# Attention in a decoder trunk: maximum, softmax, values and copies of o by halves of the queries, and Q and K of the eighth pair moved into the Q/K phase

## The chip, the cores and the metric

The kernel runs on one core of one Trainium2 chip. The core has five engines with a program each: TensorE (PE, matrix products; its weight loads are listed apart as PEld), VectorE (DVE), ScalarE (ACT), GpSimd (POOL) and SyncE (SP, which here only issues DMAs). They meet through semaphores. The metric is the device time of one execution in microseconds. A profile comes from one further execution.

## The reference

Two layers work on x of 1024 tokens × 1024 channels, in fp32: a short gated convolution and a dilated attention, each followed by a SwiGLU feed-forward (FFN). The attention has 16 heads of 64 channels. Each head has three branches (window, dilation) = (128, 1), (512, 4), (2048, 16); each branch looks back over a band of keys, with a bias by distance, and the branches are weighted by their own sums of exponentials:

```python
h = rms_norm(x, mix_norm[i])
qkv = (h @ w_qkv).reshape(bsz, seq, 3, N_HEADS, HEAD_DIM)
for window, dilation in BRANCHES:
    o, l = dilated_branch(q, k, v, rel_bias, window, dilation)   # output, log of the sum of exponentials
    ...
alpha = jax.nn.softmax(jnp.stack(lses, axis=0), axis=0)
o = jnp.sum(alpha[..., None] * jnp.stack(outs, axis=0), axis=0)
x = x + o.reshape(bsz, seq, D_MODEL) @ w_out
x = x + swiglu(rms_norm(x, ffn_norm[i]), w_gate, w_up, w_down)
```

Since the weights alpha are exponentials of the branches' log sums, the three branches are one softmax over all their keys together. The kernel computes it so: one maximum, exponentials of everything, one sum.

## The kernel before, in words

**Products in two parts.** fp32 factors are split into a high part, which ACT rounds (L145), and the low part, which DVE subtracts (L146). A product is then three matmuls: high·high, high·low, low·high. `product` (L373 to L375) does it plainly. The larger products go through `Strassen` units: seven products of combined halves in place of eight, with DVE forming the combinations of raw weights (L193), PE multiplying (L571 to L573), and ACT and DVE adding the results up into `part` (L577, L581).

**The stages.** The convolution and its FFN come first (to 938 us). Then `QueryKey.mix` computes Q and K for `QK_PAIRS = 7` of the eight pairs of heads as Strassen units (938 to 1095 us). Each result is scaled and split (L1140, L1142, L1145, L1148) and goes to DRAM by POOL's DMAs. After the first value tiles the attention runs from 1123.8 to 1412.3 us in 17 slots, and the rest of the output projection and the second FFN follow.

**A slot.** `slot(n)` (L1717) has two halves. The first does the scores of head n (L1574, L1575) in eight steps. The second does the values of head n−1 (L1647). For n up to `LAG = 13` the softmax of head n−1 runs within the first half: five subtractions of the maximum on DVE (L1636), each followed by its exponential on ACT (L1637). From slot 13 on, a head's softmax runs in the second half of its own slot, and from slot 14 on scores and values are interleaved. The maximum of a head is taken on DVE (L1599, L1620 to L1625) and over the partitions by one POOL instruction of 1024 columns (L1628). Values are accumulated in two PSUM banks, one for each half of the queries; the weights hold 64 columns of ones beside the 64 of v, so that the sums of exponentials come out in the same product. Then ACT takes the logarithm of the sums (z, L1670) and copies o (L1671), for both halves after all values.

**Names.** lf and lh are the scores of the branch of dilation 4 (lh for the second half of the queries alone), ld and lp those of the other tiles of keys (lp for the block before); ka, qa, ql are K, Q and Q's low part; kca is K by residue; vx holds the values of one pair of heads; oin is a pair's finished output read back from DRAM; x<-spill are rows of x read back.

**Dense steps.** Between the pieces of a slot a generator `fill` puts further products on PE, and the table `DENSE` gives how many of its steps each slot takes: value tiles of the groups 1 to 3 (120 steps), Q and K of pair 7 (36 steps), then the first half of the output projection, `out_product(0)` (64 steps). With the numbers of before the output projection begins in slot 12. It takes the outputs of pairs 0 to 3 as split oin, adds its results to x (L492), and loads the x rows when it first takes a weight. A slot can also take a `hook`: in slot 11 it splits the four oin.

**Orders that are fixed.** Every engine carries its instructions out in the order of the program. SP issues, among others, K and Q (L1546 to L1552), the biases (L1468, L1469), vx (L1534, L1536), oin (L1799), x rows (L1811) and raw weights (L159). `load_values` brings in vx for the two heads of a pair one after the other, into a buffer of [ones between v of the even and v of the odd head]; vx has one buffer, so the load of a head's part waits until the last values that use it.

```python
vx = scope["pool"].tile([128, 16, 192], F32, name="vx", tag="vx", bufs=1)
nc.vector.memset(vx[:, :, 64:128], 1.0)
DENSE = (13,) * 13 + (16, 13, 12, 11)
```

Of the kernel before, what the change touches and what calls it, by code (L numbers as in the profile page):

```python
# [10 lines left out]
F32 = mybir.dt.float32  # L11
# [9 lines left out]
H = 16  # L21
# [80 lines left out]
def trunk(ctx: ExitStack, tc: tile.TileContext, x, gains_in, cwi, ck, cwo, wqkv, wo, relb,  # L102
# [8 lines left out]
    def page(name, dt=F32):  # L111
        return pages.tile([128, 1024], dt, name=name, tag="page", bufs=PAGES)
# [6 lines left out]
    def bank():  # L119
        return psum.tile([128, 512], F32, name="bank", tag="bank")  # L120
# [14 lines left out]
    def split(src, dst=None, eng=nc.vector):  # L135

        w = src.shape[1]
        if dst is None:
            if w <= HALF:
                t = page("w", F32R)  # L140
                dst = t[:, :w], t[:, HALF:HALF + w]
            else:
                dst = page("w_hi", F32R)[:, :w], page("w_lo", F32R)[:, :w]
        hi, lo = dst
        nc.scalar.activation(hi, src, AF.Copy)  # L145
        eng.tensor_tensor(out=lo, in0=src, in1=hi, op=ALU.subtract)  # L146
        return hi, lo

    raw_src, raw_tile, raw_state = [], {}, [0]
    ops, made, op_state = [], {}, [0, 0]
# [13 lines left out]
    def ensure(upto):  # L166
        while op_state[0] < min(upto + 1, len(ops)):
            key = ops[op_state[0] + 1][0] if op_state[0] + 1 < len(ops) else None
            if key in sums_of:
                sums_of.pop(key)()  # L170
            made[op_state[0]] = ops[op_state[0]][1]()
            op_state[0] += 1

    def take(key, ahead=1):
        i = op_state[1]
# [1304 lines left out]
    def attention(norm, qk):  # L1480
# [47 lines left out]

        def load_values(p):
            src = vdram[p // 2]  # L1530
            for a in range(2):
                off = src.offset + p % 2 * 128 + a * 64
                dims = slice(128 * a, 128 * a + 64)
                nc.sync.dma_start(vx[:, 0:8, dims], bass.AP(src.tensor, off, [[256, 128], [128 * 256, 8], [1, 64]]))  # L1534
                for h in range(2):
                    nc.sync.dma_start(vx[:, 8 + 4 * h:12 + 4 * h, dims],  # L1536
                                        bass.AP(src.tensor, off + 512 * 256 * h, [[1024, 128], [256, 4], [1, 64]]))

        def load_kq(n):

# [20 lines left out]
        def scores(p, a, st):  # L1561
# [63 lines left out]
            nc.vector.tensor_tensor(out=m[:, HALF:], in0=m[:, HALF:], in1=lp[:, HALF:], op=ALU.max)  # L1625
            mb = page("mb")
            st["mb"] = mb
            nc.gpsimd.partition_all_reduce(mb, m, 128, bass_isa.ReduceOp.max)  # L1628
            yield

        def softmax(st):
            lf, lh, ld, lp, mb = (st[n] for n in ("lf", "lh", "ld", "lp", "mb"))
            for dst, m in ((lf, mb), (lh, mb[:, HALF:]), (ld, mb),
                           (view(lp, 8, [[32, 16], [1, 24]]), view(mb, 8, [[32, 16], [1, 24]])),
                           (lp[:, HALF:], mb[:, HALF:])):
                nc.vector.tensor_tensor(out=dst, in0=dst, in1=m, op=ALU.subtract)  # L1636
                nc.scalar.activation(dst, dst, AF.Exp)  # L1637
                yield

        def values(p, a, st):  # L1640
            lf, lh, ld, lp = (st[n] for n in ("lf", "lh", "ld", "lp"))
            acc = [bank(), bank()]
            kd = [[128, 4], [1, 32]]
            b1 = [[32, 16], [1, 8]]

            def mm(ih, off, dims, u, rhs, first=False, last=False):
                nc.tensor.matmul(view(acc[ih], off, dims), vx[:, u, 64 * a:64 * a + 128], rhs,  # L1647
                                 start=first, stop=last)

            for ih in range(2):  # L1650
# [4 lines left out]
            for r4 in range(4):  # L1655
                mm(1, r4 * 32, kd, 12 + r4, view(lh, r4 * 32, kd))
                if r4 % 2:
                    yield
            for j in range(8):
                off = (j % 4) * 8  # L1660
                mm(j // 4, off, b1, j, view(ld, blk(j), b1), last=False)
                if j:
                    mm(j // 4, off, b1, j - 1, view(lp, blk(j), b1), last=j % 4 == 3)
                yield
            o, z = st["o"], st["z"]
            n0 = slice(64 * a, 64 * a + 64)
            z0 = slice(64 - 64 * a, 128 - 64 * a)
            for ih in range(2):
                s = slice(ih * HALF, (ih + 1) * HALF)
                nc.scalar.activation(z[n0, s], acc[ih][z0], AF.Ln)  # L1670
                nc.scalar.activation(o[n0, s], acc[ih][n0], AF.Copy)  # L1671
            yield

        def finish(p):

# [38 lines left out]
        put_off, ending, due = [], [], [iter(())]  # L1714
        OZ, acts = {}, {}

        def slot(n, dense, ndense, late=0, hook=iter(())):  # L1717

            def other(k):
                for _ in range(k):  # L1720
                    next(dense, None)

            p, a = divmod(n, 2)
# [5 lines left out]
            if n + 1 < H:  # L1729
                load_kq(n + 1)  # L1730
                bias[n + 1] = load_bias(n + 1)
            if n:
# [67 lines left out]
            return raw  # L1800

        def split_attended(raw):
            return {p: split(t) for p, t in raw.items()}

        def out_product(g, ps, acts):
            for n in range(KT):
# [29 lines left out]
                        yield from value_tiles(g, j)  # L1836
            yield from out_product(0, range(AO), first)

        def halves():
            for q, t in done.items():  # L1840
                first[q] = split(t)
                yield

        dense = fill()
        for n in range(H):
# [8 lines left out]
        run(dense)  # L1854
        return acts


# [178 lines left out]
```

## Time and profile before

| | |
|---|---|
| time, median of 3 runs | 2103.54 us (2102.79 to 2103.99) |
| the profiled execution's own time | 2105.08 us |
| its span | 2103.3 us |
| Q/K phase | 938 to 1095 us |
| first value tiles | 1095 to 1123.8 us |
| attention, 17 slots | 1123.8 to 1412.3 us |
| a slot, 1 to 9 | 16.8 to 17.7 us |
| slots 10, 11, 12, 13, 14 | 18.1, 17.3, 18.9, 20.9, 19.7 us |

The profile page gives for each engine its busy time, its share of the span and its number of instructions. A row of instruction groups reads: line, engine, operation, output<-input, shape, count | total us, mean ns of one | idle time of the engine just before them, and what ended it. A row of waits reads: engine, tile and line that waited <- engine, tile and line waited for: total us, how often, the longest. A row of time stretches has for each engine the busy time and the instructions. DMA rows of SP and POOL show when the engine issued, not when the data arrived.

### The profile page before, as it was taken

What the parts mean: (1) busy time and instruction counts of PE and PEld (TensorE: products, weight loads), DVE (VectorE), ACT (ScalarE), POOL (GpSimd) and SP (SyncE); (2) the same over time, 40 slices, a digit from 0 to 9 for tenths busy, and PEclk for the clock granted to TensorE, in tenths of its full rate; (3) what the DMA queues carried; (4) which work ended last, traced back from release to release, by engine and by line L of the source; (5) the groups of instructions that cost most, each with busy time, mean ns of one, the idle gap of its engine ahead of it and who ended that gap; (6) DMA issues with size and microseconds to landing.
All of it is one profiled execution on the core that took longest, in us unless ns stands there. A gap on an engine that the chain in (4) does not pass through costs nothing. (4 is left out here: it accounts for less than half of the span.)

```text
span 2103.3 us, 30766 instructions
## 1 busy us (share of the span) xinstructions
PE 2083.1 (99%) x10990; PEld 1792.2 (85%) x10990; DVE 1746.1 (83%) x3264; ACT 1013.7 (48%) x1852; POOL 240.0 (11%) x336
## 2 busy tenths in 40 slices
PE   9999999999999999999999999999999999999998
PEld 7788888888888888887789999988788888888887
DVE  8898769988888788968984778987998888888886
ACT  7433427444444454445553566555544434456433
POOL 1000000110101010010223232211011001001000
PEclk9999999999999999999999999999999999999999
DMA  7322643233333467452658788955223323368432
GB/s 216 100 96 71 230 135 76 101 105 111 102 105 110 145 201 208 133 159 65 232 201 209 161 202 210 250 165 154 71 87 108 107 99 113 110 194 245 158 96 80
DMA packets 141495, 300.70 MB, mean 143 GB/s; under 512 B 48236, under 2 KB 54462, under 8 KB 141344
## 3 DMA queue, kind: packets, MB, share of 16 engines
q1 hardware_dynamic: 107488, 201.94, 32.4%
q0 software_dynamic: 26224, 82.11, 12.6%
q10 hardware_dynamic: 7632, 14.70, 1.9%
q8 instruction: 87, 1.43, 0.3%
q14 instruction: 64, 0.52, 0.1%
HBM read 208.42 MB, written 82.93 MB: 139 GB/s over the span
## 5 line engine op out<-in xcount | busy, mean ns | idle before, releaser
L573 PE MATMUL bank<-b,w 128*128 128x512 f32 x1980 | 772.5, 390 | 5.4 <-DVE w L146 5.2
L571 PE MATMUL bank<-b,w 128*128 128x512 f32 x1980 | 772.3, 390 | 2.3 <-ACT w L145 1.1
L572 PE MATMUL bank<-b,w 128*128 128x512 f32 x1980 | 771.9, 390 | 0.6 <-DVE b L882 0.6
L573 PEld LDWEIGHTS bank<-b,w 128*128 128x128 f32 x1980 | 372.0, 188 | 87.5 <-DVE w L146 10.5
L571 PEld LDWEIGHTS bank<-b,w 128*128 128x128 f32 x1980 | 372.3, 188 | 80.3 <-ACT w L145 1.9
L572 PEld LDWEIGHTS bank<-b,w 128*128 128x128 f32 x1980 | 372.3, 188 | 76.6 <-DVE b L882 1.2
L145 ACT ACTIVATE w<-combo 128x512 fp32r<-128x512 f32 (+2 forms) x492 | 251.5, 541 | 238.9 <-DVE combo L193 219.7
L146 DVE TENSOR_TENSOR w<-combo,w 128x512 fp32r<-128x512 f32 (+2 forms) x492 | 279.8, 582 | 37.8 <-ACT w L145 37.0
L577 ACT ACTIVATE part<-bank 128x512 f32<-128x512 f32 x189 | 112.5, 595 | 383.9 <-PE bank L573 378.7
L146 DVE TENSOR_TENSOR w<-raw,w 128x512 fp32r<-128x512 f32 (+2 forms) x345 | 194.4, 585 | 36.5 <-ACT w L145 36.5
L581 DVE TENSOR_TENSOR part<-part,bank 128x256 f32<-128x256 f32 (+1 forms) x369 | 173.1, 499 | 31.9 <-PE bank L573 17.3
L145 ACT ACTIVATE w<-raw 128x512 fp32r<-128x512 f32 (+2 forms) x345 | 168.5, 531 | 47.8 <-PE bank L573 12.2
L373 PE MATMUL bank<-w_hi,w 128*128 128x512 f32 (+1 forms) x400 | 151.0, 378 | 0.1
L375 PE MATMUL bank<-w_hi,w 128*128 128x512 f32 (+1 forms) x400 | 149.3, 373 | 0.7 <-DVE w L146 0.7
L374 PE MATMUL bank<-w_lo,w 128*128 128x512 f32 (+1 forms) x400 | 149.0, 373 | 0.0
L801 DVE TENSOR_TENSOR x<-x,bank 128x512 f32<-128x512 f32 x136 | 92.9, 683 | 28.7 <-PE bank L573 28.7
L492 DVE TENSOR_TENSOR x<-x,bank 128x512 f32<-128x512 f32 (+1 forms) x104 | 66.7, 644 | 59.8 <-PE bank L375 58.9
L193 DVE TENSOR_TENSOR combo<-raw 128x512 f32<-128x512 f32 (+1 forms) x174 | 112.6, 648 | 0.0
L375 PEld LDWEIGHTS bank<-w_hi,w 128*128 128x128 f32 x400 | 75.3, 188 | 14.8 <-DVE w L146 1.6
L564 DVE TENSOR_TENSOR b<-hin,b 128x512 fp32r<-128x512 f32 x126 | 79.5, 686 | 9.4 <-ACT b L563 9.4
L373 PEld LDWEIGHTS bank<-w_hi,w 128*128 128x128 f32 x400 | 75.5, 189 | 12.3 <-ACT w L145 0.5
L374 PEld LDWEIGHTS bank<-w_lo,w 128*128 128x128 f32 x400 | 75.5, 189 | 11.9
(234 smaller groups left out, 3377.0 us busy)
## 6 DMA issues: line engine op xcount, KB each, us to landing
hin<-part SPq DMA_DIRECT2D x126, 256.0 KB
raw<-in_ffn_w_gate SPq DMA_DIRECT2D x44, 512.0 KB
raw<-in_ffn_w_up SPq DMA_DIRECT2D x44, 512.0 KB
part<-sum POOLq DMA_DIRECT2D x72, 256.0 KB, 2.3
raw<-in_ffn_w_down SPq DMA_DIRECT2D x48, 384.0 KB
raw<-in_attn_w_qkv SPq DMA_DIRECT2D x27, 512.0 KB
raw<-in_conv_w_in SPq DMA_DIRECT2D x24, 512.0 KB
part<-part POOLq DMA_DIRECT2D x36, 256.0 KB, 2.6
```

The costliest lines, as they stand in the source:

```text
L145: nc.scalar.activation(hi, src, AF.Copy)
L146: eng.tensor_tensor(out=lo, in0=src, in1=hi, op=ALU.subtract)
L193: eng.tensor_tensor(out=c, in0=a, in1=b, op=op)
L373: nc.tensor.matmul(b, whi[:, a], ahi[:, s], start=first, stop=False)
L374: nc.tensor.matmul(b, whi[:, a], alo[:, s], start=False, stop=False)
L375: nc.tensor.matmul(b, wlo[:, a], ahi[:, s], start=False, stop=last)
L571: nc.tensor.matmul(b, hi[:, a], bhi, start=start and k == 0, stop=False, skip_group_check=True)
L572: nc.tensor.matmul(b, hi[:, a], blo, start=False, stop=False, skip_group_check=True)
L573: nc.tensor.matmul(b, lo[:, a], bhi, start=False, stop=k == n - 1, skip_group_check=True)
L577: nc.scalar.activation(t, b, AF.Copy)
L581: nc.vector.tensor_tensor(out=t, in0=t, in1=b, op=ALU.add)
L801: nc.vector.tensor_tensor(out=X[n][:, half(h)], in0=X[n][:, half(h)], in1=b, op=ALU.add)
```

## The change

- `QK_PAIRS` is 8: the Q/K phase does the eighth pair as an eighth Strassen unit, and the 36 dense steps of pair 7 leave `fill`. `DENSE` has new numbers (184 steps in all), and the output projection's first half now begins in slot 11.
- The oin of pairs 0 and 1 are loaded and split in slot 9, those of pairs 2 and 3 in slot 10 (`OIN`), after the slot's K, Q and bias loads.
- The all-reduce of the maximum is two instructions of 512 columns, the first issued as soon as half a of the queries has its maximum. The softmax has seven steps of at most 512 columns, half a first, where there were five.
- The values do half a of the queries to its end, with its z and o, and then half b.
- vx is laid out as [ones, v of the even head, v of the odd head] repeated, so z and o change places, and both heads' values come in three DMAs with rows of 512 bytes, where there were six with rows of 256.
- During the attention a split's low part is not issued at once but put on a list, which is emptied ahead of the next dense step (`flush_lows`).

```diff
-QK_PAIRS = 7
+QK_PAIRS = 8
-FILL = (("v", 0), ("v", 1), ("v", 2), ("v", 3), ("qk", 7))
-DENSE = (13,) * 13 + (16, 13, 12, 11)
+FILL = (("v", 0), ("v", 1), ("v", 2), ("v", 3))
+OIN = LAG - 3
+DENSE = (11,) * 9 + (10, 10) + (11, 11, 14, 10, 10, 9)
...
-        eng.tensor_tensor(out=lo, in0=src, in1=hi, op=ALU.subtract)
+        low = lambda: eng.tensor_tensor(out=lo, in0=src, in1=hi, op=ALU.subtract)
+        if behind[0]:
+            lows.append(low)
+        else:
+            low()
...
+        flush_lows()
         ensure(i + ahead)
+        if i + 1 > state0:
+            flush_lows()
...
-        vx = scope["pool"].tile([128, 16, 192], F32, name="vx", tag="vx", bufs=1)
-        nc.vector.memset(vx[:, :, 64:128], 1.0)
+        vx = scope["pool"].tile([128, 16 * 192 + 64], F32, name="vx", tag="vx", bufs=1)
+        nc.vector.memset(view(vx, 0, [[192, 17], [1, 64]]), 1.0)
...
-            for a in range(2):
-                off = src.offset + p % 2 * 128 + a * 64
-                dims = slice(128 * a, 128 * a + 64)
-                nc.sync.dma_start(vx[:, 0:8, dims], bass.AP(src.tensor, off, [[256, 128], [128 * 256, 8], [1, 64]]))
-                for h in range(2):
-                    nc.sync.dma_start(vx[:, 8 + 4 * h:12 + 4 * h, dims],
-                                        bass.AP(src.tensor, off + 512 * 256 * h, [[1024, 128], [256, 4], [1, 64]]))
+            off = src.offset + p % 2 * 128
+            nc.sync.dma_start(view(vx, 64, [[192, 8], [1, 128]]),
+                              bass.AP(src.tensor, off, [[256, 128], [128 * 256, 8], [1, 128]]))
+            for h in range(2):
+                nc.sync.dma_start(view(vx, (8 + 4 * h) * 192 + 64, [[192, 4], [1, 128]]),
+                                  bass.AP(src.tensor, off + 512 * 256 * h, [[1024, 128], [256, 4], [1, 128]]))
...
+                    mb = page("mb")
+                    st["mb"] = mb
+                    nc.gpsimd.partition_all_reduce(mb[:, :HALF], m[:, :HALF], 128, bass_isa.ReduceOp.max)
                 yield
...
-            nc.gpsimd.partition_all_reduce(mb, m, 128, bass_isa.ReduceOp.max)
+            nc.gpsimd.partition_all_reduce(mb[:, HALF:], m[:, HALF:], 128, bass_isa.ReduceOp.max)
...
-            for dst, m in ((lf, mb), (lh, mb[:, HALF:]), (ld, mb),
+            a, b = half(0), half(1)
+            for dst, m in ((lf[:, a], mb[:, a]), (ld[:, a], mb[:, a]),
                            (view(lp, 8, [[32, 16], [1, 24]]), view(mb, 8, [[32, 16], [1, 24]])),
-                           (lp[:, HALF:], mb[:, HALF:])):
+                           (lf[:, b], mb[:, b]), (lh, mb[:, b]), (ld[:, b], mb[:, b]), (lp[:, b], mb[:, b])):
...
             for ih in range(2):
+                acc[ih] = bank()
                 for r4 in range(4):
...
+                for r4 in range(4 * ih):
+                    mm(1, r4 * 32, kd, 12 + r4, view(lh, r4 * 32, kd))
...
+                for j in range(4 * ih, 4 * ih + 4):
...
+                nc.scalar.activation(z[n0, half(ih)], acc[ih][n0], AF.Ln)
+                nc.scalar.activation(o[n0, half(ih)], acc[ih][o0], AF.Copy)
                 yield
...
-            if n == LAG - 2:
-                done.update(load_attended(range(AO)))
-            hook = halves() if n == LAG - 2 else iter(())
-            slot(n, dense, DENSE[n], 3 if n == H - 2 else 0, hook)
+            ps = {OIN - 1: (0, 1), OIN: (2, 3)}.get(n, ())
+            hook = halves(ps)
+            slot(n, dense, DENSE[n], 3 if n == H - 2 else 0, hook, ps)
```

On SP, this is slot 11 before, from the next head's K (ka) to the x rows, which slot 12's first dense step asks for:

```order
L1546 DMA ka<-kq_1_2926 64x1024
L1547 DMA ka<-kq_1_2926 64x1024
L1534 DMA vx<-vdram_95 128x8x64
L1536 DMA vx<-vdram_95 128x4x64 x2
L1534 DMA vx<-vdram_95 128x8x64
L1536 DMA vx<-vdram_95 128x4x64 x2
L1551 DMA qa<-kq_0_2925 64x1024 x2
L1552 DMA ql_10192<-kq_0_2925 64x1024
L1468 DMA bias<-tables 128x1x361
L1469 DMA bias<-tables 128x1x349
```

```order
L1551 DMA qa<-kq_0_2925 64x1024 x2
L1552 DMA ql_10193<-kq_0_2925 64x1024
L1468 DMA bias<-tables 128x1x361
L1469 DMA bias<-tables 128x1x349
L1811 DMA x<-spill_77 128x1024
L1811 DMA x<-spill_78 128x1024
L1811 DMA x<-spill_79 128x1024
```

Between the two pieces stand only the two loads of the next slot's ka. After, the same place:

```order
L1559 DMA ka<-kq_1_2926 64x1024
L1560 DMA ka<-kq_1_2926 64x1024
L1546 DMA vx<-vdram_95 128x8x128
L1549 DMA vx<-vdram_95 128x4x128 x2
L1564 DMA qa<-kq_0_2925 64x1024 x2
L1565 DMA ql_10353<-kq_0_2925 64x1024
L1482 DMA bias<-tables 128x1x361
L1483 DMA bias<-tables 128x1x349
L1829 DMA x<-spill_77 128x1024
L1829 DMA x<-spill_78 128x1024
L1829 DMA x<-spill_79 128x1024
```

The vx loads are three in place of six, and the x rows stand right behind the second bias, one slot's loads earlier.

On ACT, this is the end of slot 13 before: the softmax of head 13, then z and o of head 12's values, one pair of rows for each half of the queries:

```order
L1637 ACTIVATE lf<-lf 128x1024
L1637 ACTIVATE lh<-lh 128x512
L1637 ACTIVATE ld<-ld 128x1024
L1637 ACTIVATE lp<-lp 128x16x24
L1637 ACTIVATE lp<-lp 128x512
L145 ACTIVATE w<-raw 128x512
L1670 ACTIVATE z<-bank 64x512
L1671 ACTIVATE o<-bank 64x512
L1670 ACTIVATE z<-bank 64x512
L1671 ACTIVATE o<-bank 64x512
```

After, the same place:

```order
L1684 ACTIVATE z<-bank 64x512
L1685 ACTIVATE o<-bank 64x512
L1652 ACTIVATE lf<-lf 128x512
L1652 ACTIVATE ld<-ld 128x512
L1652 ACTIVATE lp<-lp 128x16x24
L1652 ACTIVATE lf<-lf 128x512
L1652 ACTIVATE lh<-lh 128x512
L1652 ACTIVATE ld<-ld 128x512
L1652 ACTIVATE lp<-lp 128x512
L146 ACTIVATE w<-raw 128x512
L1684 ACTIVATE z<-bank 64x512
L1685 ACTIVATE o<-bank 64x512
```

The first pair of z and o, that of half a, now stands ahead of the exponentials; the second is still behind them.

More of the change, by code (lines that the diff above doesn't have):

```diff
@@ L145, in split, with flush_lows @@
         nc.scalar.activation(hi, src, AF.Copy)
-        eng.tensor_tensor(out=lo, in0=src, in1=hi, op=ALU.subtract)
+        low = lambda: eng.tensor_tensor(out=lo, in0=src, in1=hi, op=ALU.subtract)
[3 more added lines that the diff above has]
+            low()
         return hi, lo
+    behind, lows = [False], []
+    def flush_lows():
+        while lows:
+            lows.pop(0)()
     raw_src, raw_tile, raw_state = [], {}, [0]
@@ L174, in take @@
     def take(key, ahead=1):
-        i = op_state[1]
+        i, state0 = op_state[1], op_state[0]
         assert ops[i][0] == key, (ops[i][0], key)
+        flush_lows()
         ensure(i + ahead)
+        if i + 1 > state0:
+            flush_lows()
         op_state[1] += 1
@@ L1641, in values @@
             lf, lh, ld, lp = (st[n] for n in ("lf", "lh", "ld", "lp"))
-            acc = [bank(), bank()]
+            acc = {}
             kd = [[128, 4], [1, 32]]
@@ L1654, in values @@
                         yield
-            for r4 in range(4):
-                mm(1, r4 * 32, kd, 12 + r4, view(lh, r4 * 32, kd))
-                if r4 % 2:
-                    yield
[L1659 to L1663, printed above, removed]
-                yield
[L1665 to L1672, printed above, removed]
+                for r4 in range(4 * ih):
+                    mm(1, r4 * 32, kd, 12 + r4, view(lh, r4 * 32, kd))
+                    if r4 % 2:
+                        yield
+                for j in range(4 * ih, 4 * ih + 4):
+                    off = (j % 4) * 8
+                    mm(ih, off, b1, j, view(ld, blk(j), b1), last=False)
+                    if j:
+                        mm(ih, off, b1, j - 1, view(lp, blk(j), b1), last=j % 4 == 3)
+                    yield
+                nc.scalar.activation(z[n0, half(ih)], acc[ih][n0], AF.Ln)
+                nc.scalar.activation(o[n0, half(ih)], acc[ih][o0], AF.Copy)
+                yield
         def finish(p):
@@ L1715, in attention, with slot @@
         OZ, acts = {}, {}
-        def slot(n, dense, ndense, late=0, hook=iter(())):
+        def slot(n, dense, ndense, late=0, hook=iter(()), ps=()):
             def other(k):
                 for _ in range(k):
+                    flush_lows()
                     next(dense, None)
@@ L1731, in slot @@
                 bias[n + 1] = load_bias(n + 1)
+            done.update(load_attended(ps))
             if n:
@@ L1802, in split_attended @@
         def split_attended(raw):
-            return {p: split(t) for p, t in raw.items()}
+            done = {p: split(t) for p, t in raw.items()}
+            flush_lows()
+            return done
         def out_product(g, ps, acts):
@@ L1837, in fill, with halves @@
             yield from out_product(0, range(AO), first)
-        def halves():
-            for q, t in done.items():
-                first[q] = split(t)
+        def halves(ps):
+            for q in ps:
+                first[q] = split(done.pop(q))
                 yield
         dense = fill()
+        behind[0] = True
         for n in range(H):
-            if n == LAG - 2:
-                done.update(load_attended(range(AO)))
-            hook = halves() if n == LAG - 2 else iter(())
-            slot(n, dense, DENSE[n], 3 if n == H - 2 else 0, hook)
+            ps = {OIN - 1: (0, 1), OIN: (2, 3)}.get(n, ())
+            hook = halves(ps)
+            slot(n, dense, DENSE[n], 3 if n == H - 2 else 0, hook, ps)
             run(hook)
@@ L1854, in attention @@
         run(dense)
+        flush_lows()
+        behind[0] = False
         return acts
```

7 lines of the change are left out of this document (4 added, 3 removed).

## The prediction

> **What bounds the kernel now.** I read the page's busy times first, then the stretches of time one by one, then the waits of TensorE (PE) in the attention, and last the chain of work there.
>
> ```profile
> span 2103.3 us, 30766 instructions
> PE 2083.1 (99%) x10990; PEld 1792.2 (85%) x10990; DVE 1746.1 (83%) x3264; ACT 1013.7 (48%) x1852; POOL 240.0 (11%) x336
> ```
>
> PE is busy for 99% of the span, so the first question is how many matmuls the change leaves, and the second whether PE comes to wait. The stretches that the change touches (PE, weight loads, VectorE, ScalarE, GpSimd busy; clock; DMA share; GB/s):
>
> ```profile
> core 0: us, PE busy (x) PEld busy (x) DVE busy (x) ACT busy (x) POOL busy (x), PEclk, DMA share, GB/s
> 980.00:1060.00 80.00, 79.22 (x346) 64.22 (x345) 78.61 (x125) 46.00 (x80) 19.77 (x36) 1.00 0.56 184
> 1060.00:1095.00 35.00, 35.00 (x156) 29.01 (x155) 28.61 (x45) 17.64 (x31) 7.58 (x14) 1.00 0.53 196
> 1123.77:1412.32 288.55, 287.76 (x2225) 275.79 (x2224) 234.35 (x420) 166.29 (x233) 78.64 (x59) 1.00 0.78 195
> 1308.33:1325.64 17.31, 17.31 (x120) 15.88 (x119) 16.53 (x27) 13.19 (x17) 5.13 (x3) 1.00 1.13 256
> 100.00:150.00 50.00, 50.00 (x222) 41.42 (x221) 47.64 (x97) 18.90 (x33) 2.51 (x5) 1.00 0.25 75
> ```
>
> The first two are the Q and K phase, the third the attention, the fourth its slot 11, the fifth an early stretch for comparison: there DVE is 95% busy and PE doesn't wait. In the attention PE is idle for 288.55 − 287.76 = 0.79 us, and there is one wait:
>
> ```profile
> PE bank L1574 <- ACT o L1671: 0.8, 1, 0.8
> ```
>
> A matmul's recorded length is not its price. In the chain of work, nine matmuls of 512 columns fill the time from 1401.87 to 1403.91, 2.04 / 9 = 0.227 us each, while the page's mean of one is 390 ns:
>
> ```profile
> L571 PE MATMUL bank<-b,w 128*128 128x512 f32 x1980 | 772.3, 390 | 2.3 <-ACT w L145 1.1
> 1401.87 0.23 PE bank L373
> ...
> 1403.91 0.04 issue
> ```
>
> [...]
>
> **Q and K of the eighth pair.** Before, that pair runs in the attention as plain split products:
>
> ```profile
> L373 PE MATMUL bank<-b,w_hi 128*128 128x512 f32 x32 | 13.4, 419 | 0.0
> L375 PE MATMUL bank<-b,w_lo 128*128 128x512 f32 x32 | 12.6, 393 | 0.0
> ```
>
> With L374 these are 3 × 32 = 96 matmuls of 512 columns, 96 × 0.227 = 21.8 us. After, the pair is an eighth unit of the phase: 7 products × 4 inner tiles × 3 = 84 matmuls, 84 × 0.227 = 19.1 us. The phase grows, the attention shrinks, and the net is −12 × 0.227 = **−2.7 us**. It must not be lost to DVE in the phase. These are the groups of 938 to 1095 us:
>
> ```profile
> L146 DVE TENSOR_TENSOR w<-combo,w 128x512 fp32r<-128x512 f32 x28 | 19.1, 683 | 1.2 <-ACT w L145 1.1
> L146 DVE TENSOR_TENSOR w<-raw,w 128x512 fp32r<-128x512 f32 x25 | 16.7, 686 | 0.9 <-ACT w L145 0.9
> L193 DVE TENSOR_TENSOR combo<-raw 128x512 f32<-128x512 f32 x14 | 9.5, 682 | 0.0
> L581 DVE TENSOR_TENSOR part<-part,bank 128x512 f32<-128x512 f32 x19 | 12.9, 681 | 4.8 <-ACT part L577 4.0 <-PE bank L573 0.7
> L1140 DVE TENSOR_TENSOR kq<-part,rstd 128x512 f32<-128x512 f32 x12 | 12.6, 1052 | 0.1
> ```
>
> The eighth unit adds 4 low parts of combinations, 3 of raw weights, 4 combinations and 3 additions, and on its way out 2 of the 1.05 us products (L1140) and 6 instructions of the 0.68 us class (two L1142, four L1148): 20 × 0.684 + 2 × 1.052 = 15.8 us of DVE beside 19.1 us of PE, 83%. That is the share of the second stretch (28.61 of 35), where PE never waits; I put it at 0. The first stretch (78.61 of 80 us, PE short of 0.78) says that the margin is small in the middle of the phase. If the eighth unit ran there, the cost would be that shortfall scaled by 19.1/80, 0.2 us: the bounds are 0 and 0.2.
>
> In the attention the same move takes off four emissions of that kind (2 × 1.05 + 6 × 0.68 = 6.2 us) and two low parts of 1024 columns (2.4 us), 8.6 us of DVE in all.
>
> **Maximum and softmax in halves.** The 16 heads' groups in the attention:
>
> ```profile
> L1628 POOL PARTITION_ALL_REDUCE mb<-m x16 | 55.9, 3496 | 142.8 <-DVE m L1625 81.7 <-PE bank L1647 22.9 <-PE bank L1519 14.0
> L1636 DVE TENSOR_TENSOR lf<-lf,mb 128x1024 f32<-128x1024 f32 x16 | 19.6, 1224 | 32.9 <-POOL mb L1628 32.9
> L1636 DVE TENSOR_TENSOR lh<-lh,mb 128x512 f32<-128x512 f32 x16 | 10.9, 683 | 0.0
> L1637 ACT ACTIVATE lf<-lf 128x1024 f32<-128x1024 f32 x16 | 17.0, 1060 | 33.7 <-DVE lf L1636 33.7
> L1637 ACT ACTIVATE lh<-lh 128x512 f32<-128x512 f32 x16 | 10.1, 628 | 5.6 <-DVE lh L1636 5.6
> ```
>
> Two halves of 0.683 take 0.142 us more than one whole of 1.224, and two exponentials of 0.628 take 0.196 more than 1.060. There are 32 such pairs (lf and ld of 16 heads): +4.5 us on DVE, +6.3 on ACT. With the 8.6 us gone DVE ends with less than before (234.35 + 4.5 − 8.6 = 230 us) in a stage that is 22 us shorter, 86% on average, and ACT at about 65%. In the slots with the adds to x, DVE stays near the 95% of slot 11 now (16.53 of 17.31), where PE doesn't wait either. GpSimd's all-reduce of a half is not in the trace: between half of 3.50 us and all of it, 32 times, so +0 to +56 us beside 78.64 of 289. It is hidden for all heads up to the twelfth, whose softmax runs a slot later. Late heads gain, since half a is reduced while half b is still being scored. All of this I put at 0.
>
> **The copies of o.** The one wait of the attention, in the chain of work:
>
> ```profile
> 1366.82 0.61 ACT lp L1637
> 1367.43 0.52 ACT w L145
> 1367.95 0.48 ACT z L1670
> 1368.44 0.60 ACT o L1671
> 1369.05 0.04 issue
> 1369.09 0.33 PE bank L1574
> ```
>
> The scores of head 14 need a bank that the copies of head 12's values hold, and ACT gets to them only behind the exponentials of head 13. After, z and o of half a stand ahead of all seven exponentials, and the chain's first release comes some 4 us earlier: **−0.8 us**. If the same bank is then held by half b, which stays behind them, nothing is gained; bounds −0.8 and 0. I take −0.8, because the bank asked for first is the one released first.
>
> **The rows of x.** The output projection's first half starts a slot earlier, and its first x rows are loaded by SP in slot 11 behind other loads. Before:
>
> ```profile
> 1307.82 1.63 SPq L1534 DMA_DIRECT2D vx<-vdram  x1
> 1315.95 0.55 SPq L1469 DMA_DIRECT2D bias<-tables  x1
> 1324.11 2.74 SPq L1811 DMA_DIRECT2D x<-spill  x3
> 1325.64 0.37 PE L1574 MATMUL bank<-qa,kca 128*128 128x256 f32 x1
> 1337.02 0.68 DVE L492 TENSOR_TENSOR x<-x,bank 128x512 f32<-128x512 f32 x1
> ```
>
> The x rows are issued 1.5 us before slot 12 opens (1325.64) and are added 11.4 us after it; nothing waits. After, they are issued right behind the second bias of slot 11, some 8 us after the slot opens, and DVE's add stands at about +8.5 to +12. It waits there for the landing, and the subtractions of half b, whose exponentials the values need, are queued behind it on DVE. SP's landings aren't in the page; GpSimd's reach from 2.3 us at the median for small pieces to 9.2 us for other x rows of the same 512 KB:
>
> ```profile
> part<-sum POOLq DMA_DIRECT2D x72, 256.0 KB, 2.3
> ...
> x<-spill POOLq DMA_DIRECT2D x16, 512.0 KB, 9.2
> ```
>
> So the rows land between +10 and +17. PE's next values need half b's exponentials at about +14, that is the add done by about +11: bounds 0 and 6 us for PE. I take **+0.5**, near the low end, because the load that is issued at 1324.11 now lands in a queue as full as that of slot 11 and no wait shows at 1337.02, and because most landings in this range (up to 3 us) end inside the slack.
>
> **vx in one piece.** Before, one half of vx is fetched while the other is still in use; now all of it follows the last values of an odd head. In slots 1 to 13 the next values come some ten us later (1307.4 to 1318.31 in slot 11), and the whole megabyte (1.05 MB) at slot 11's 256 GB/s takes 4.1 us and 2.3 or more to land. The tight place is slot 14 to 15:
>
> ```profile
> 1377.11 0.38 SPq L1534 DMA_DIRECT2D vx<-vdram  x1
> 1377.54 1.26 SPq L1536 DMA_DIRECT2D vx<-vdram  x2
> 1385.56 0.83 PE L1647 MATMUL bank<-lf,vx 128*128 128x128 f32 x6
> ```
>
> 8.4 us of cover before; after, eight dense steps of 3 × 0.227 us and the first scores leave about 5.9, against 1.05 MB / 195 GB/s (third stretch) = 5.4 and 2.3 to land: at most 1.8 us too late. The lower bound is 0, and I take **+0.3**: the first values need tiles 8 to 11 alone, the second of the load's three pieces. The low parts that are issued a step later are 0: PE waits for none of them in the attention now, and those of a step are made before its product takes them.
>
> **Sum.** −2.7 − 0.8 + 0.5 + 0.3 = −2.7 us. The profiled execution took 2105.08 us (span 2103.3 and 1.8 around it), 1.5 above the median of 2103.54; the difference goes off the median: **2100.8 us**, −0.13%. A measurement of this kernel can tell about 0.2% (4.2 us) from no change, so the likeliest verdict is "within".
>
> **Rivals.** (1) Matmuls in the attention cost more than the steady pace, as the 419 ns of the first of each dense step (against 393 of the third) may hint: at the recorded 390 to 419 ns the twelve are worth 4.7 to 5.0 us, and with the wait gone and none new it is 2103.54 − 5.6 = 2097.9. Against it: the starts are 0.227 us apart. (2) The x rows come at their upper end: −3.5 + 6 + 0.3 = +2.8, 2106.3. For it speaks slot 11, where the DMA engines' share is 1.13. (3) Slower: the one-piece vx load doesn't fit its cover. It decides where a load takes longer than the ten us of slots 9, 11 and 13, that is below some 130 GB/s; 2.5 us late in each of the three and 1.8 in slot 15 are 9.3 − 3.5 = +5.8, 2109.3. For it: one issue takes SP 1.63 us there (1307.82), so the queue is full. Against it: the same bytes pass now, in rows twice as long. [...]
>
> **How the numbers follow.** Forecast (2099.4 to 2103) 0.47; first rival 0.25, with 0.03 from the forecast's edge where all gains come and PE's other idle moments shrink; second 0.10; third 0.15. Faster by over 0.2% 0.28, within 0.55, slower 0.17. The range leaves out half of the first rival and most of the third: 2098.3 to 2106.5.
>
> **What would show it.** After: the phase up to the first scores longer by 19 us, the attention shorter by 22; the wait of L1574 for o gone; DVE's L492 add of slot 11 waiting for x; PE waiting for vx at the first values of head 14, if anywhere. A wait of over 2 us at values in slots 9 to 13, or a DVE without a gap there and PE behind it, would make the prediction wrong.

## The result, and the profile after

The changed kernel takes 2107.11 us (median of 20 runs, 2105.36 to 2111.2), the kernel before 2103.45 us (20 runs, 2102.22 to 2104.99). The ratio is 1.0018, 95% interval 1.0013 to 1.0024: 3.7 us **slower**, where 2.7 us faster was forecast.

The page of the changed kernel begins:

```profile
span 2105.1 us, 30800 instructions
PE 2080.8 (99%) x10978; PEld 1790.0 (85%) x10978; DVE 1760.2 (84%) x3308; ACT 1020.9 (48%) x1892; POOL 250.1 (12%) x352
```

The twelve matmuls are gone (10978 for 10990), and DVE has 14 us more to do. The two profiled spans differ by 1.8 us only, because the execution of before that was profiled lost 2 us in its first stage, ahead of anything changed. An estimated 1.7 us of that is PE's clock: the stretches of 2 us from 8 to 14 us of that profile show a granted clock of 0.75, 0.50 and 0.90, those of after 1.00. The timelines of PE show where the two kernels differ: the same instruction near the start of the Q/K phase, and the same one in the second FFN, in before

```profile
941.10 0.50 PE L373 MATMUL bank<-w_hi,w 128*128 128x512 f32 x1
...
1488.60 0.50 PE L571 MATMUL bank<-b,w 128*128 128x512 f32 x1 [0.41 <-ACT part L577]
```

and after:

```profile
939.10 0.50 PE L387 MATMUL bank<-w_hi,w 128*128 128x512 f32 x1
...
1490.23 0.50 PE L585 MATMUL bank<-b,w 128*128 128x512 f32 x1 [0.42 <-ACT part L591]
```

Between them lie 547.50 us before and 551.13 after: +3.6 us in these two executions, as much as the difference of the medians. So the loss lies between the start of the Q/K phase and the start of the second FFN, and there PE now waits. Its waits from 930 to 1480 us (total, times, longest):

```profile
PE bank L1662 <- ACT ld L1652: 2.0, 1, 2.0
PE bank L585 <- ACT part L591: 1.3, 1, 1.3
PE bank L1662 <- ACT lp L1652: 1.0, 2, 0.8
PE bank L585 <- ACT w L146: 0.6, 1, 0.6
PE bank L587 <- DVE w L147: 0.6, 1, 0.6
PE bank L1587 <- ACT kca L1571: 0.2, 1, 0.2
```

The fourth and fifth stood in the profile before too, in the Q/K phase. The wait for the copy of o is gone, as forecast. New are a wait of 1.3 us for a copy (part, at 1092, when ten of the phase's 56 products are left, just ahead of the eighth unit's first), 0.2 us for kca, and the last exponentials, ld and lp, for the values (L1662). The longest is in slot 11. The chain of work there:

```profile
1313.14 5.66 DMA vx<-vdram
1318.80 0.02 issue
1318.81 9.27 DMA x<-spill
1328.08 0.02 issue
1328.10 0.69 DVE x L506
1328.79 0.60 DVE ld L1651
1329.39 0.34 DVE ld L1624
1329.73 0.33 DVE lp L1629
1330.06 0.61 DVE lp L1651
1330.67 0.02 issue
1330.69 0.64 ACT lp L1652
1331.33 0.04 issue
1331.38 2.29 PE bank L1662 x14
```

The x rows are issued at 1318.81, 5.5 us after the slot opened (1313.27), land 9.3 us later, and the add stands on DVE until then. Behind it are the subtractions of ld and lp of half b. Before, in slot 12, the add did not wait, and one piece of the softmax stood behind it:

```profile
1337.02 0.68 DVE L492 TENSOR_TENSOR x<-x,bank 128x512 f32<-128x512 f32 x1
1337.61 0.69 DVE L1636 TENSOR_TENSOR lp<-lp,mb 128x512 f32<-128x512 f32 x1
```

After, DVE's row of waits and the stretches after it (PE, weight loads, DVE, ACT, POOL busy, clock, DMA share, GB/s):

```profile
DVE x L506 <- DMA x<-spill: 4.2, 1, 4.2
```

```profile
1328.00:1330.00 2.00, 0.11 (x1) 0.00 (x0) 1.90 (x5) 0.57 (x1) 0.00 (x0) 1.00 1.03 411
1330.00:1332.00 2.00, 1.11 (x7) 0.92 (x8) 1.97 (x6) 1.36 (x4) 0.00 (x0) 1.00 1.09 269
1332.00:1334.00 2.00, 2.00 (x13) 1.90 (x13) 2.00 (x3) 2.00 (x3) 1.39 (x1) 0.64 1.05 221
1334.00:1336.00 2.00, 2.00 (x8) 1.73 (x7) 2.00 (x4) 1.95 (x4) 0.96 (x2) 0.50 1.00 226
```

After PE's two waits (2.0 and 0.8 us) its granted clock falls to 0.64 and 0.50 for about 4 us. That costs an estimated 2 × 0.36 + 2 × 0.50 = 1.7 us on top. The sum of the profile: −2.7 for the matmuls, −0.8 for o, +1.3 at 1092, +3.0 for the exponentials, +0.2 for kca, +1.7 for the clock: +2.7. The remaining 0.9 of the 3.6 us is not in any row of waits; part of it is the first matmul after a wait: at 1092.00, in the chain below, it takes 0.50 us in place of 0.23.

### The profile page after: what moved, and what is told of

Same layout as the page of the kernel before. It is cut to its first block, busy times and chain, and to the rows that moved or that the text cites. A ratio compares the mean times of both kernels' runs of the same rounds, so it can differ in the third digit from the quotient of the medians.

```text
span 2105.1 us, 30800 instructions
## 1 busy us (share of the span) xinstructions
PE 2080.8 (99%) x10978; PEld 1790.0 (85%) x10978; DVE 1760.2 (84%) x3308; ACT 1020.9 (48%) x1892; POOL 250.1 (12%) x352
## 4 chain that ended last, share of the span: by engine, by line
PE 48%; DVE 4%; ACT 1%; DMA 1%; issue 0%; DVEq 0%; ACTq 0%
PE bank L587 9%; PE bank L585 9%; PE bank L586 9%; PE bank L1662 4%; PE bank L387 2%; PE bank L389 2%; PE bank L388 2%; PE bank L1531 1%; PE bank L677 1%; PE bank L1533 1%; PE bank L1532 1%; PE bank L680 1%; PE bank L679 1%; PE bank L1588 1%; PE bank L1587 1%; DVE w L147 1%
## 5 line engine op out<-in xcount | busy, mean ns | idle before, releaser
L587 PE MATMUL bank<-b,w 128*128 128x512 f32 x2008 | 782.6, 390 | 4.8 <-DVE w L147 4.5
L585 PE MATMUL bank<-b,w 128*128 128x512 f32 x2008 | 782.7, 390 | 4.4 <-ACT w L146 2.2
L586 PE MATMUL bank<-b,w 128*128 128x512 f32 x2008 | 782.1, 390 | 0.6 <-DVE b L896 0.6
L587 PEld LDWEIGHTS bank<-b,w 128*128 128x128 f32 x2008 | 376.9, 188 | 88.1 <-DVE w L147 9.9
L585 PEld LDWEIGHTS bank<-b,w 128*128 128x128 f32 x2008 | 377.2, 188 | 82.7 <-ACT w L146 3.3
L586 PEld LDWEIGHTS bank<-b,w 128*128 128x128 f32 x2008 | 377.2, 188 | 78.1 <-DVE b L896 1.2
```

The source lines that it names most:

```text
L585: nc.tensor.matmul(b, hi[:, a], bhi, start=start and k == 0, stop=False, skip_group_check=True)
L586: nc.tensor.matmul(b, hi[:, a], blo, start=False, stop=False, skip_group_check=True)
L587: nc.tensor.matmul(b, lo[:, a], bhi, start=False, stop=k == n - 1, skip_group_check=True)
```

## The experiments

All times are medians of 11 runs (e4: of 5) beside runs of the kernel before on the same chip. d is the difference to it; the changed kernel has d = +3.7. The intervals reach some 0.0009 to each side, that is 1.9 us, so a difference of a microsecond between two edits is not shown by the medians alone.

| run | edit to the changed kernel | us | d | ratio, 95% interval |
|---|---|---|---|---|
| e1 | x rows loaded in slot 10 | 2104.86 | +1.2 | 1.0007 (0.9998 to 1.0016) |
| e2 | last operand of the Q/K phase a unit later | 2106.13 | +2.5 | 1.0012 (1.0004 to 1.0021) |
| e3 | vx in six pieces | 2104.24 | +0.6 | 1.0007 (0.9999 to 1.0016) |
| e4 | eighth pair back among the dense steps | 2110.73 | +7.1 | 1.0034 (1.0021 to 1.0046) |
| e5 | e1 and e2 | 2103.27 | −0.1 | 1.0001 (0.9992 to 1.0010) |
| e6 | two pieces of softmax in each of the first two steps | 2101.93 | −1.4 | 0.9995 (0.9986 to 1.0004) |
| e7 | e1, e2 and e6 | 2100.91 | −2.4 | 0.9988 (0.9979 to 0.9997) |
| e8 | e4 and e6 | 2104.31 | +1.0 | 1.0003 (0.9994 to 1.0012) |
| e9 | softmax in its five pieces of before | 2102.90 | −0.8 | 0.9997 (0.9987 to 1.0006) |
| e10 | e2 and e6 | 2100.70 | −3.0 | 0.9987 (0.9979 to 0.9996) |
| e11 | e10, low parts at once | 2101.66 | −2.0 | 0.9993 (0.9984 to 1.0001) |
| e12 | e10, vx in six pieces | 2100.47 | −3.2 | 0.9987 (0.9978 to 0.9996) |

**e1: the x rows earlier.**

```diff
+OIN, X_AT = LAG - 3, 10
...
             done.update(load_attended(ps))
+            if n == X_AT:
+                load_x(0)          # the first three rows, as out_product loads them
```

> The changed kernel, with the first three rows of x loaded in slot 10 (behind oin), not when the output projection takes its first weight in slot 11. Theory A (x rows late): the wait of 4.2 us for x in slot 11 goes, with PE's two waits there (2.0 and 0.8 us) and the matmuls at a lowered clock behind them: 4 to 4.5 us faster than the changed kernel, about 2102.8. Theory B (the halved softmax makes DVE the bound of the attention): the wait goes over to a DVE operation that waits for nothing, PE still waits in slot 11, and the time stays within 1 us of 2107.1. Theory C (vx in one piece delays the loads): the x rows are on time, and vx or K is late instead.

2.4 us of the 3.7 go, not 4 to 4.5. The wait for x is gone, and the clock stays up (1.00 in the three stretches of 2 us from 1311), but PE still waits 1.0 us for lp and 0.3 for ld, now in slot 10, where DVE is held by something else: its maximum waits for a page that an output on its way to DRAM still holds.

```profile
DVE m L1613 <- DMA odram<-o: 2.1, 1, 2.1
```

None of the three theories had that. Late x rows are one occasion of the wait and not the only one.

**e2: the last operand of the Q/K phase.** The phase's hooks name the unit of pair 5, the last but one of seven; the change to eight units left them.

```diff
-{(1, 2): gather, (3, 1): spread, (5, 1): load, (5, 7): last_operand}
+{(1, 2): gather, (3, 1): spread, (6, 1): load, (6, 7): last_operand}
```

> The changed kernel, with the load and the split of the last operand of the Q/K phase moved from the unit of pair 5 to that of pair 6, so that it comes in the last unit but one again, as before the change. Theory A (the eighth unit is short of pages, since the last operand's four pages are taken a unit too early): PE's wait of 1.25 us at 1092 for a copy that stands behind a split waiting for a page goes: 1.4 us faster than the changed kernel, about 2105.7. If the stall came from ACT's or DVE's load in the eighth unit, it stays: 2107.1.

PE's wait at 1092 is gone from the trace, and that is what shows the cause. The median falls by 1.2 us (d from +3.7 to +2.5); the same edit takes off 1.3 and 1.5 us in e5 and e10 below. In the changed kernel the chain there reads

```profile
1090.52 0.24 PE bank L587
...
1090.83 0.63 ACT w L146
1091.46 0.49 ACT part L591
1091.96 0.04 issue
1092.00 0.50 PE bank L585
```

and ACT's timeline says what the split waited for:

```profile
1090.83 0.63 ACT L146 ACTIVATE w<-raw 128x512 fp32r<-128x512 f32 x1 [4.57 <-PE bank L587]
```

The page that the split writes was the one a matmul had just read. ACT stood there for 4.6 us, without work, and the copy that PE waits for stood behind the split.

**e3: vx in six pieces.**

```diff
-            off = src.offset + p % 2 * 128
-            nc.sync.dma_start(view(vx, 64, [[192, 8], [1, 128]]), ...)
+            for a in range(2):
+                off = src.offset + p % 2 * 128 + a * 64
+                nc.sync.dma_start(view(vx, 64 + 64 * a, [[192, 8], [1, 64]]), ...)
...
```

> The changed kernel, with vx loaded in six pieces of 256-byte rows again, those of the even head first, in the new layout. Theory C (the one-piece load holds SP's queue, so that the x rows are issued late): the x rows are issued some 3 us earlier and PE's wait in slot 11 shrinks by 2 to 3 us, 2104 to 2105. Theory A (their place in SP's order is too late in any case): three more issues stand ahead of the x rows, the wait is the same or up to 2 us longer, 2107 to 2109.

3.1 us of the 3.7 go. Taken alone that speaks for the one-piece load as the cause, and for the first piece of the chain above (5.66 us of vx ahead of x). But the x rows are not issued earlier, as theory C has it: SP issues them at 1321.61, 7.0 us after slot 11 opened (1314.60), where the changed kernel took 5.5. DVE waits 3.9 us for them, and PE nearly as long as in the changed kernel (1.7 and 0.8 us for ld and lp in slot 11). What differs behind the waits is the clock:

```profile
1331.00:1333.00 2.00, 1.12 (x7) 0.93 (x8) 1.97 (x6) 1.37 (x4) 0.00 (x0) 1.00 1.08 335
1333.00:1335.00 2.00, 2.00 (x17) 1.87 (x16) 2.00 (x3) 2.00 (x3) 1.40 (x1) 1.00 1.04 199
```

Here it stays at 1.00. The execution that was profiled (2106.13) is 1.9 us above the median of e3, so what the median gained is not in this trace. Run e12 asks about the load itself.

**e4: the eighth pair back among the dense steps.**

```diff
-QK_PAIRS = 8
+QK_PAIRS = 7
-FILL = (("v", 0), ("v", 1), ("v", 2), ("v", 3))
+FILL = (("v", 0), ("v", 1), ("v", 2), ("v", 3), ("qk", 7))
-DENSE = (11,) * 9 + (10, 10) + (11, 11, 14, 10, 10, 9)
+DENSE = (13,) * 13 + (16, 13, 12, 11)
```

> The changed kernel, with Q and K of the eighth pair back among the dense steps and the step table of before, so that the output projection begins in slot 12; halves, vx, oin and low parts as changed. Theory A: no page shortage in the phase, x rows on time, and the 12 matmuls back: 2107.1 - 1.5 - 4.4 + 2.7 = 2103.9, within 1 us. Theory B: the halves still cost, and with the emissions back on DVE more than now: over 2106.

This was the run that overthrew theory A. The x rows are on time and the phase is as before, and the kernel is 7.1 us slower than before. PE waits for the same two exponentials, in four slots (2, 5, 10 and 11), first at 1165 us, long before any x row is used:

```profile
PE bank L1662 <- ACT lp L1652: 4.0, 4, 1.5
PE bank L1662 <- ACT ld L1652: 1.5, 2, 0.7
```

DVE's timeline at the first of these:

```profile
1163.48 1.22 DVE L147 TENSOR_TENSOR w_lo<-raw,w_hi 128x1024 fp32r<-128x1024 f32 x1 [2.99 <-PE bank L1532]
1164.62 0.68 DVE L1651 TENSOR_TENSOR ld<-ld,mb 128x512 f32<-128x512 f32 x1
1165.22 0.42 DVE L1624 TENSOR_TENSOR ld<-bank,bias 128x256 f32<-128x256 f32 x1
1165.56 0.42 DVE L1629 TENSOR_TENSOR lp<-bank,bias 128x256 f32<-128x256 f32 x1
1165.89 0.68 DVE L1651 TENSOR_TENSOR lp<-lp,mb 128x512 f32<-128x512 f32 x1
```

Here DVE waits for a page that a matmul reads (3.0 us), and again the last two subtractions stand behind it. That gave theory D: a slot gives out one piece of the softmax in each of its first steps; five pieces were through after the fifth step, seven need the seventh. Whatever DVE waits for in the middle of a slot (x, a page, a low part) now has two pieces behind it that the values need soon.

**e6: two pieces in each of the first two steps.**

```diff
                 for i in range(8):
                     next(due[0], None)
+                    if i < 2:
+                        next(due[0], None)
                     next(sc, None)
```

> The changed kernel, with two pieces of the softmax in each of the first two steps of a slot, so that all seven have been issued after the fifth step, as the five before the change. Theory D (the seven pieces reach two steps further down the slot, so that two of them stand behind whatever DVE waits for in its middle): in slot 11 only lp of half b, or nothing, stands behind the add to x; PE's wait there is 1 to 2 us shorter and its clock stays up, 2.5 to 4 us faster than the changed kernel, 2103 to 2104.6. If only the lateness of x counts, PE waits as long as before: 2106.5 to 2107.5.

5.1 us faster than the changed kernel, more than expected. DVE waits for x nearly as long as before the edit; only the order has changed:

```profile
1320.86 0.68 DVE L1651 TENSOR_TENSOR ld<-ld,mb 128x512 f32<-128x512 f32 x1
...
1322.13 0.68 DVE L1651 TENSOR_TENSOR lp<-lp,mb 128x512 f32<-128x512 f32 x1
...
1328.31 0.69 DVE L506 TENSOR_TENSOR x<-x,bank 128x512 f32<-128x512 f32 x1 [3.64 <-DMA x<-spill]
```

In slots 9 to 16 PE is left with one wait:

```profile
PE bank L1587 <- ACT kca L1571: 0.2, 1, 0.2
```

So here a DVE held for 3.6 us costs PE nothing, with nothing that PE needs behind it. That the gain is above the 4.5 us that slot 11 cost (2.8 of waits, an estimated 1.7 of clock) fits the smaller wait for lp (0.3 us at 1247 in the changed kernel), which is gone too, and the slow first matmul behind a wait (0.50 us for 0.23 at 1092.00 in the changed kernel).

**e8: the same edit where x plays no part**, that is e4 and e6 together.

> The kernel with Q and K of the eighth pair back among the dense steps (2110.7), with two pieces of the softmax in each of the first two steps. Theory D: PE's 5.5 us of waits for ACT's last two exponentials in four slots go nearly all, 2105 to 2106.5. If they come from DVE's load alone, the waits stay: 2110 to 2111.

6.1 us of e4's 7.1 go, and no wait for exponentials is left in the trace. What is left in the attention is one wait of 1.5 us for kca, at the end of slot 10, where ACT copies kca behind the split of an oin. Beside e6 this run also tests the count of the matmuls, since the place of the eighth pair (with its step table) is all that differs: d is 2.4 us higher, near the 2.7 of the count (e8's wait for kca and e6's at 1092 nearly cancel).

**e9: the five pieces of before.**

```diff
-            for dst, m in ((lf[:, a], mb[:, a]), (ld[:, a], mb[:, a]),
+            for dst, m in ((lf, mb), (lh, mb[:, HALF:]), (ld, mb),
                            (view(lp, 8, [[32, 16], [1, 24]]), view(mb, 8, [[32, 16], [1, 24]])),
-                           (lf[:, b], mb[:, b]), (lh, mb[:, b]), (ld[:, b], mb[:, b]), (lp[:, b], mb[:, b])):
+                           (lp[:, HALF:], mb[:, HALF:])):
```

> The changed kernel with the softmax in its five pieces of before (three of 1024 columns' width or less ahead of half b's), all else as changed. Theory D (the two more pieces of the softmax, at one per step, are what PE waits for): DVE waits for x as long as now, nothing of the softmax stands behind it, and 4 to 5 us of the changed kernel's time go: 2102 to 2103. If the halves themselves are harmless and only x counts: 2106 to 2107.

As theory D has it, by undoing the one part of the change itself. DVE waits 3.2 us for x here, without effect on PE: the last piece (lp, at 1323.37) stands ahead of the add (1329.09). e9 also has less work on DVE (1748.8 us busy against 1760.2 in the changed kernel), which could have been the gain; but e6 has 1761.2 and gains as much. PE is left with 1.2 us for kca in slot 10 and 0.3 for an exponential at 1402.

**e5, e7 and e10: do the gains add?**

> The first two edits together: x rows in slot 10, the last operand of the Q/K phase a unit later. If the two waits are independent their gains add: 2104.9 - 1.4 = 2103.5.

> x rows in slot 10, the last operand a unit later, and two pieces of the softmax in each of a slot's first two steps. Theory D: the waits of the values for ACT's last exponentials (1.2 + 0.3 us with the x rows early) go too: 2102 to 2102.5, 1 us or more under the kernel before, which is the sum of the prediction without its new waits. If those waits have another cause: 2103.5.

> Two pieces of the softmax in each of the first two steps, and the last operand a unit later; x rows as in the changed kernel. Theory D: with the softmax out of the way the late x rows are worth nothing, so this is as fast as with the x rows moved too: 2101.9 - 1.4 = 2100.5, within 0.7 us of the kernel with all three edits (2100.9).

They do where they are independent: the last operand's place takes 1.3 us off e1 (e5) and 1.5 off e6 (e10). With the softmax out of the way no gain from the place of the x rows is seen (e7, which has them early, is 0.5 us behind e10 by d, 0.2 by the times themselves). e10 is the best of these with the fewest edits: 3.0 us under the kernel before, ratio 0.9987 (0.9979 to 0.9996). PE's waits from 930 to 1480 us in it are the two that the Q/K phase had before:

```profile
PE bank L585 <- ACT w L146: 0.6, 1, 0.6
PE bank L587 <- DVE w L147: 0.6, 1, 0.6
```

**e11 and e12: two parts that the prediction put near nothing.** e11 keeps `behind[0]` false, so each low part is issued at once; e12 has e3's edit.

> The kernel of the last run, with each low part issued at once, as before the change. If the low parts' place is worth nothing, as the prediction had it: within 0.5 us of the last run. If DVE's wait for ACT's high part (11 us of DVE's time in the attention before) counted: up to 2 us slower.

> The kernel of the last but one run, with vx in six pieces of 256-byte rows again. The six pieces made the changed kernel 2.9 us faster. Theory D: only because the x rows landed a little sooner and PE's clock stayed up; with nothing behind the x rows the gain is gone, within 0.6 us of the kernel with three pieces. If the one-piece load costs by itself: 1 to 3 us faster than that.

e12 finds no cost of the load of vx by itself: −0.2 us, well within the interval, where the same edit was worth 3.1 in the changed kernel. That it mattered there by when x landed, and by the clock, is argued, not shown. The execution of e12 that was profiled (2103.21) is 2.7 us above its median: an oin landed 10.3 us after its issue, its split held kca on ACT in slot 10, and PE waited 2.3 us there, with a granted clock of 0.63 and 0.52 in the two stretches of 2 us behind it (from 1298 us). The place of the oin in slots 9 and 10, for which the prediction has no term, was not tested by a run of its own, and the waits for kca (0.2 to 2.3 us in most of these runs, in e8 and e12 behind the split of an oin) stay open. e11 is 1.0 us slower than e10, with a wait of 0.9 us for an exponential at 1382; the intervals overlap, so a gain of up to a microsecond from the later low parts is possible and not shown.

## Why the prediction was wrong

- **The count** (−2.7) was right. In e10's profile the time from the phase's first old wait to the first score is 19.1 us longer than before (170.63 against 151.55), and from there to the second FFN 23.1 us shorter (341.71 against 364.83); forecast were 19.1 and 21.8 + 0.8. e8 against e6 fits: +2.4. By the medians e10 comes to −3.0, where −2.7 and −0.8 are −3.5.
- **The copies of o** (−0.8) were right: the row is gone.
- **"Maximum and softmax in halves ... All of this I put at 0"** is the step that failed: a cost of 4.4 to 5.1 us was put at nothing. It added up the microseconds of two halves against one whole (they fit) and took "it is hidden" from busy shares. It never asked in which step of the slot the last of seven pieces is issued, when each step issues one. (Its paragraph on x says that half b's subtractions are queued behind the add, but not that they are there only because there are seven pieces.) The two steps' delay is harmless by itself, but it moves ld and lp of half b behind any wait that DVE has in the middle of a slot. e6, which changes that alone, takes off 5.1 us, and e9, which undoes the seven pieces, 4.4. The sign that the prediction named for being wrong came: PE's waits at the values of slot 11 are 2.8 us.
- **The x rows** (+0.5, bounds 0 and 6) had the right mechanism, place and queue, and the wrong value in the range: issue at 5.5 us into the slot (some 8 was forecast), landing after 9.3 (the far end of the landings quoted), DVE held for 4.2 us, PE for 2.8, and an estimated 1.7 more for the clock, 4.5 in all. This is the same loss as that of the halves, seen from the other side, and not to be added to it: in e6 DVE still waits 3.6 us for x, and PE does not wait. The reason given for the low value, that no wait showed at 1337.02, proved nothing: before, the rows had 13 us from issue to use. And that half b's subtractions stand behind the add was the prediction's own sentence; two of them did.
- **The eighth unit** (0, bounds 0 and 0.2) cost 1.3 us by the trace, 1.2 to 1.5 by three pairs of medians, just ahead of its own products. It was costed by DVE's load, but DVE was not what PE waited for: it stood idle there for 2.5 us itself, waiting for ACT. Pages were short, because the last operand's four pages are taken at a fixed unit. e2 removes the wait.
- **vx in one piece** (+0.3, and the third rival's place) showed no cost of its own: no run's trace has PE waiting for vx, and e12 shows no gain from undoing it.
- **The rivals.** The outcome is nearest to the second (the x rows at their upper end, 2106.3), given 0.10; it had no place for the wait at 1092, nor for the lost clock. The third had the sign right and the mechanism wrong. For the first nothing speaks: with the waits gone e10 stands at 2100.7, and the 96 matmuls that left the attention were worth about the 0.227 us each of the forecast.
- **The clock.** The forecast has no term for a fall of PE's clock. The changed kernel's trace has one, to 0.64 and 0.50, behind idle pieces of 2.0 and 0.8 us in slot 11. And the profile that the prediction was made from has a fall too, at 9 us (0.50 from 10 to 12 us), and in the 7 us before it no wait of PE is over 0.6 us.

## What to carry to other kernels

When one instruction is cut into several that are issued one per step of a schedule, count the step in which the last is issued, and list what its engine may be waiting for by then. A wait on an engine that is not the bottleneck is free only as long as nothing that the bottleneck needs stands behind it: DVE's wait for x cost PE nothing at 3.6 us in e6, and 2.8 us at 4.2 in the changed kernel. When a loop gains an iteration, look for hooks tied to a fixed iteration number.

## What was not expected of the hardware

PE's granted clock fell behind some waits of a few microseconds and not behind others. In the changed kernel it fell to 0.50 behind 2.0 and 0.8 us of waiting within 3.3 us (1328.1 to 1331.4), in e12 to 0.52 behind one wait of 2.3 us; in e3 it stayed at 1.00 behind 1.7 and 0.8 us. Behind the longest wait, 3.7 us in e2, it stayed down longest:

```profile
1327.00:1331.00 4.00, 0.27 (x3) 0.08 (x1) 1.98 (x5) 0.63 (x1) 0.00 (x0) 0.98 1.07 348
1331.00:1333.00 2.00, 1.51 (x5) 1.22 (x6) 1.97 (x5) 1.40 (x3) 0.00 (x0) 0.50 1.02 213
```

The missing clock of such a fall adds up to an estimated 1.7 us in the changed kernel and in e12, and to 3.3 in e2 (0.50 in three stretches of 2 us, 0.83 in a fourth). So e12's one wait of 2.3 us comes to an estimated 4.0, and the changed kernel's two, of 2.8 together, to 4.5; which waits bring a fall is not settled by these traces. The runs of the changed kernel spread over 5.8 us and those of before over 2.8, and the clock goes with it: the four longest (2108.5 to 2111.2) had a mean granted clock of 0.995 to 0.997, the three shortest 0.998 or 0.999. One thousandth of the clock is an estimated 2.1 us of this kernel. What held PE in those executions no trace shows.

In the changed kernel, DVE's subtractions of the maximum are slow where they run wholly within one of GpSimd's all-reduces: the mean of lf's halves is 845 ns, where lh's, of the same shape, is 682.

```profile
L1651 DVE TENSOR_TENSOR lf<-lf,mb 128x512 f32<-128x512 f32 x32 | 27.1, 845 | 0.0
...
L1651 DVE TENSOR_TENSOR lh<-lh,mb 128x512 f32<-128x512 f32 x16 | 10.9, 682 | 0.0
```

Seven of lf's 32 took 1.16 or 1.53 us, and each of these ran wholly within an all-reduce; every one of lf's that met an all-reduce only in part took 0.68 or 0.69. A slowed one did not last to the all-reduce's end: the subtraction that began at 1198.76, within an all-reduce, ended at 1200.29, the all-reduce at 1200.48. Why they are slowed is not shown. e9 takes the overlap away: there the subtractions start when both halves are reduced (DVE waits 25.0 us for the second), and lf's, whole again, have a mean of 1224 ns, as before the change. The prediction's +4.5 us for the halved subtractions left this out: lf and ld come to 50.6 us in place of 39.1, +11.5. It is not the main thing that PE waited for, since e10 has more of it (55.8 us) and PE doesn't wait for the softmax; a slowed ld (1.53 us) stands in the chain of the small wait at 1247.
